# Layer planner: split window of 7 steps, longer estimate for small-row DMAs, eighth accumulator held back

## The chip, the core and the metric

The kernel runs on one core of a Trainium2 chip. The core has TensorE (matmuls and transposes, into the 8 banks of PSUM), VectorE, ScalarE and GpSimd (elementwise work), and DMA queues that are fed from SyncE, ScalarE and GpSimd. Each engine takes its instructions in the order of its own queue; semaphores hold an instruction until its inputs are there. In the profile PE is TensorE, DVE is VectorE, ACT is ScalarE, POOL is GpSimd and SP is SyncE. The metric is the device time of one execution in microseconds (us); lower is better.

## The reference

One encoder layer on 256 tokens of width 2048, all in float32: two kinds of attention side by side on one input projection, an output projection, and a gated feed-forward part of width 5632, with a layer norm at each seam.

```python
h = layer_norm(x, ln_in_g, ln_in_b)
proj = einsum('bsd,de->bse', h, w_in[l])                  # 2048 x 6144
na_out = neighbourhood_attention(na_q, na_k, na_v, na_rpb[l])   # 8 heads of 128
diff_out = differential_attention(d_q, d_k, d_v, lam, rel_bias_table)  # 4 heads of 256
diff_out = rms_norm(diff_out, diff_subln_g[l]) * (1.0 - lambda_init)
mixed = einsum('bse,ed->bsd', concatenate([na_out, diff_out]), w_out[l])
h = layer_norm(DEEPNORM_ALPHA * h + mixed, ln1_g[l], ln1_b[l])
ffn = einsum('bsf,fd->bsd', silu(h @ w_gate[l]) * (h @ w_up[l]), w_down[l])
h = layer_norm(DEEPNORM_ALPHA * h + ffn, ln2_g[l], ln2_b[l])
```

## The kernel before

**Units and splits.** Every weight matrix is read once, in units of 128 rows by 1024 columns (512 KB). A float32 product is made from three fast products: each operand is split into a high part (a copy to the `fp32r` type on ScalarE, `split_hi`, L406) and a low part (a subtraction on VectorE, `split_lo`, L410), and high x high, high x low and low x high are added in PSUM. So each unit costs ScalarE and VectorE one 128x1024 instruction each, and one slot of the 46 in the pool `slab` becomes two.

**Stages.** The units go in this order: six groups of 16 for the input projection (differential query, key, value, then neighbourhood query, key, value), two groups of 16 for the output projection (`o`, beginning with the rows of the differential attention), 16 units for one block of the gate and up matrices (`f`), ten groups of 16 for the rest of gate and up (`g`, `u`), and two groups of 44 for the down projection (`d`). For the first 144 units a *step* is one unit times one half of the tokens: six matmuls of 512 columns into two banks. `steps` (L1392) writes out the order. The first eight units of the input projection and of `f` are "whole" steps for the first half of the tokens: they multiply in float32 directly and need no split (two slower matmuls).

**Blocks of seven products.** From `g` on the work goes in blocks of two units by both token halves. A plain block has eight products (three matmuls each). A block listed in `SEVEN` or `SEVEN_D` (L38, L39) is done with seven products instead, from sums and differences of its parts, which are further work for VectorE and ScalarE (`seven_parts`, L1019; `add_mid_sums`, L1093). Seven products have seven accumulators; in the down projection a plain block has the accumulators 2, 3, 4 and 8, so both kinds together fill all eight banks. The product list of each block is in `products` (L1136); products 6 and 7 of a plain down block go to accumulator 8, and product 6 of a block of seven to accumulator 4.

**The planner.** The program is written out by a planner that runs when the kernel is built. `Timed` (L67) keeps an estimated clock for each engine and estimated times at which tiles are written and read; `note` (L98) adds each instruction's estimated cost. For a DMA issued on GpSimd it counts 1.05 us of issue, the transfer, and 1.2 + 2.0 us behind it. Work that is not a step of the main chain (layer norms, attention, the transposes of the gated result `mid_side`, L970) is a *side task*: a generator that yields the engine and the tiles that it wants next. In the main loop (L1535 to L1555), for each step:

- `load` issues weight loads up to 7 units ahead of the step's unit (8 in the blocks) on SP;
- the splits of the next `URGENT` = 3 steps are written out whatever they wait for;
- `side.elementwise` writes out side work for VectorE, ScalarE and GpSimd as long as that engine's clock is less than `BACKLOG` = 3 us past TensorE's;
- `next_part` writes out splits (and sums) for the units of the `window`, the next `AHEAD_S` = 24 steps, if their inputs are ready by the estimate, the engine is at most 2 us past TensorE, and slots are free (six more must stay free for units beyond the nearest);
- `side.best` puts side matmuls and transposes ahead of the step if their inputs and a bank have been ready for `SLACK` = 1.6 us by the estimate, or if the step is not `possible` yet.

An instruction, once written out, holds its place in its engine's queue, whatever the real times are.

**Around the change.** The neighbourhood attention loads a bias for each of its eight heads with four DMAs of 64 floats a row from GpSimd into a ring `nb` of two buffers (`na_bias`, L898); a `min` on VectorE takes it from there (`na_head`, L911) and frees the buffer. The same ring takes the transposed gated result: `mid_side` does four transposes into a bank, copies the bank to `nb` on ScalarE and stores that from GpSimd into `mid_d` in DRAM, from which the down projection reads it back. At the end of the last `u` group four such tasks are left. `take_product` (L1194) takes a bank for each accumulator when its first product comes; `Step.possible` (L1480) says when a step may go.

Of the kernel before, what the change touches and what calls it, by code (L numbers as in the profile page):

```python
# [35 lines left out]
NSG = 5  # L36
SLOTS = 46
SEVEN = (0, 2, 4, 6)  # L38
SEVEN_D = (range(0, 20, 3), range(20, 5, -3))  # L39
AGAIN = 3  # L40


class Engine:
# [21 lines left out]
class Timed:  # L65
# [32 lines left out]
    def note(self, name, op, outs, ins):  # L98
        n = max(int(np.prod([c for _, c in list(x.ap)[1:]])) for x in outs + ins)
        start = self.ready(*ins)  # L100
        for w, r, c in map(self.times, outs):
            start = max(start, float(r[c].max()), float(w[c].max()) if name != "pe" and op != "dma_start" else 0.0)
        if op == "dma_start":
            dims = [c for _, c in list(outs[0].ap)]
            rows = np.prod(dims[:-1])
            if name in self.clock:
                start = self.clock[name] = max(self.clock[name], start) + (1.05 if name == "pool" else 0.1)
            end = max(self.clock["dma"], start) + float(max(rows * dims[-1] * 4 / 360e3, rows * 0.0026))
            self.clock["dma"] = end
            end += self.LATENCY["dma"] + (2.0 if name == "pool" else 0.0)  # L110
            name = "dma"
        else:
            first = str(ins[0].dtype) if ins else ""
            wide = any("PSUM" in str(getattr(x.tensor, "_space", "")) for x in ins)
            m = int(np.prod([c for _, c in list(outs[0].ap)[1:]]))
            if name == "pe":
                if op == "transpose":
                    cost = 0.108
                elif first.endswith("float32"):
                    cost = m / 600 + 0.005  # L120
                else:
                    cost = m / 2400 + 0.0135
            elif name == "act":
                cost = 0.1 + n / 1200
            elif name == "dve":
                fast = op in ("tensor_scalar", "tensor_copy") and not wide
                cost = 0.07 + n / (1920 if fast else 960)
            else:
                cost = 0.1 + n / 400
            end = max(self.clock[name], start) + cost  # L130
        if name != "dma":
            self.clock[name] = end
            end += self.LATENCY[name]
        for w, r, c in map(self.times, ins):
            r[c] = np.maximum(r[c], end)
        for w, r, c in map(self.times, outs):
            w[c] = end
# [114 lines left out]
def layer_kernel(ctx: ExitStack, tc: tile.TileContext, A: dict, out: bass.AP):  # L252
# [39 lines left out]
    def used(key, n, *tiles):  # L292

        uses[key] = uses.get(key, 0) + 1
        if uses[key] == n:
            leave(*tiles)
# [31 lines left out]
    units = []  # L328
# [14 lines left out]
    hT, mixT, h1T, mid = {}, {}, {}, {}  # L343
# [13 lines left out]
    for n in range(2):  # L357
        ks = range(KF) if n == 0 else [k + i for k in range(KF - 2, -1, -2) for i in range(2)]
        add_group(("d", n), ks, [W_D[:, n * 1024 : (n + 1) * 1024]], mid, SEVEN_D[n])
    U = len(units)  # L360
# [6 lines left out]
    def splits_mid(u):  # L367


        g, k = units[u]["group"], units[u]["k"]  # L370
        return g == ("d", 0) and k % 4 == 0 or g == ("d", 1) and k % 4 == 2 and k // 4 < AGAIN

    def load(u):
# [11 lines left out]
        if splits_mid(u):  # L385
# [3 lines left out]
            nc.sync.dma_start(mid_whole[c], mid_d[c * P : (c + 1) * P, :])  # L389
        elif un["group"] == ("d", 1) and un["seven"] and un["k"] % 2 == 0 and un["k"] // 4 >= AGAIN:  # L390
            i = un["k"] // 2
# [24 lines left out]
    def tokens(x, t):  # L416

        return x[:, t] if len(x.shape) == 3 else x[:, t * P : (t + 1) * P]
# [42 lines left out]
    L2 = 8  # L461
    R0 = 3
    R1 = 8
    AHEAD = 7
# [47 lines left out]
    side = Side(nc, banks)  # L512
    have = {}
# [469 lines left out]
    def used_mid(c):  # L983
        n = 0 if ("mid 1", c) not in have else 1
        used(("mid", n, c), 1 + sum(i // 2 == c for i in SEVEN_D[n]), mid_whole[c])

# [106 lines left out]
    def add_mid_sums(u, parts):  # L1093

        i = units[u]["k"] // 2
        c = i // 2
        first = units[u]["group"][1] == 0 or c < AGAIN
        x = mid_whole[c][:, :, i % 2 * 2 : i % 2 * 2 + 2] if first else mid_pair[i]
# [37 lines left out]
    def products(u):  # L1136

        k = units[u]["k"]
        i = k // 2

        def x(row, t):
            return lambda: tuple(tokens(p, t) for p in units[u]["lhs"][k + row])

        def f(m):
            return lambda: forms[u if is_down(u) else i][m]

        def b(row, col):
            return lambda: w_block(u, row, col)

        def t13(m):  # L1150
            return lambda: (sums[u]["hi"][:, m], sums[u]["lo"][:, m])

        def t24(n):
            return lambda: (sums[u][2][:, n // 4], sums[u][4][:, n // 4])

        a_, b_, c_, d_ = x(0, 0), x(1, 0), x(0, 1), x(1, 1)
        if units[u]["seven"]:
            def b11():
                return sums[u]["b11"][:, 0], sums[u]["b11"][:, 1]

            return [
                (1, a_, b11),
                (2, b_, b(1, 0)),
                (3, f(2), b(1, 1)),
                (5, f(3), t13(0)),
                (7, f(0), t13(1)),
                (6, f(1), t24(2)),
                (4, d_, t24(4)),
            ]
        if is_down(u):  # L1170
            return [
                (2, a_, b(0, 0)),
                (2, b_, b(1, 0)),
                (3, a_, b(0, 1)),
                (3, b_, b(1, 1)),
                (4, c_, b(0, 0)),
                (4, d_, b(1, 0)),
                (8, c_, b(0, 1)),
                (8, d_, b(1, 1)),
            ]  # L1180
        return [
            (2, a_, b(0, 0)),
            (2, b_, b(1, 0)),
            (3, f(0), b(0, 1)),
            (3, f(1), b(1, 1)),
            (5, c_, b(0, 1)),
            (5, d_, b(1, 1)),
            (4, c_, b(0, 0)),
            (4, d_, b(1, 0)),
        ]  # L1190

    q, part, gate = {}, {}, {}

    def take_product(u, n):  # L1194
# [11 lines left out]
        if over:  # L1206
# [5 lines left out]
            if is_down(u):  # L1212
                if u in form_tiles:
                    leave(form_tiles[u])
                if name[1] == 1 and k % 4 == 0 or name[1] == 0 and k % 4 == 2 and k // 4 < AGAIN:
                    leave(*mid_tiles.pop(k // 4))
# [177 lines left out]
    def steps():  # L1394

        t1 = 0
        for u in range(SG):
            f = u < NF0 or FFN <= u < FFN + NF1  # L1400
            yield 0, u, f
            if f:
                continue
            if u < FFN - 40:
                behind = max(1, NF0 - (u - NF0) // R0)
            elif u < FFN:
                behind = max(1, L1 - (FFN - 1 - u) // 3) if u < FFN - 1 else 0
            else:
                behind = SG - 1 - u
            while t1 <= u - behind:  # L1410
                yield 1, t1, False
                t1 += 1
        for u in range(SG, U, 2):
            for n in range(4 if u >= U - L2 else len(products(u))):
                yield u, n

    def last_steps():
# [23 lines left out]
    def emit_part(o):  # L1441
        o["fn"]()
        o["done"] = True
# [16 lines left out]
    class Step:  # L1460
# [18 lines left out]
        def possible(self):  # L1479
            if self.kind == "product":  # L1480
                k = units[self.u]["k"]
                if is_down(self.u):

                    return ("mid", k // 4, 0) in have and (k > 2 or self.n < 6 or not side.tasks)
                return ("forms", k // 2) in have and all(("1", t, k // 4) in have for t in range(2))
            return possible(self.t, self.u, self.f)

# [47 lines left out]
    for i, step in enumerate(order):  # L1535
        step.load()
        window = order[i : i + AHEAD_S]
        for s in window[:URGENT]:
            s.finish_parts()
        coming = list(dict.fromkeys(p for s in window for p in s.parts if p[0] in raw and (not p[1] or p[0] + 1 in raw)))  # L1540
        near = {p for s in window[: AHEAD_N if step.kind == "product" else AHEAD] for p in s.parts}
        for _ in range(8):
            now = nc.clock["pe"]
            side.elementwise(now, BACKLOG)
            o = next_part(coming, near, now)
            while o is not None:
                emit_part(o)
                o = next_part(coming, near, now)
            task, when = side.best()
            main = nc.ready(*step.operands()) if step.possible() else 1e9  # L1550
            if task is None or when >= 1e8 or (when + SLACK > now and when + SLACK > main):
                break
            side.advance(task)
        step.operands()
        step.emit()  # L1555
# [45 lines left out]
```

## Time and profile before

| | before |
|---|---|
| time, median of 3 runs | 1139.98 us (1139.0 to 1140.16) |
| profiled execution: time | 1139.54 us |
| profiled execution: span | 1137.7 us |
| busy: TensorE | 1113.4 us (98%) |
| busy: TensorE weight load | 906.4 us (80%) |
| busy: VectorE | 932.1 us (82%) |
| busy: ScalarE | 601.2 us (53%) |
| busy: GpSimd | 60.3 us (5%) |
| mean granted clock of TensorE | 0.997 |
| DMA | 237.15 MB, mean 208 GB/s |

The span runs from the first to the last instruction; the time of the same execution is 1.84 us longer. All instructions carry the line of the helper that records them (L52), so they are told apart by their tiles: `sl` is a slot of the pool (weights, splits, activations), `acc` a bank of PSUM, `nb` and `s` are rings, `ident` is the identity for transposes. In a timeline the brackets show how long the engine stood idle before an instruction and what released it. A PE line `acc<-sl,sl` of 512 columns is a matmul of the main chain, `acc<-ident,...` is a transpose; a DVE or ACT line `sl<-sl` of 128x1024 is a split (in the blocks also a sum's). A few matmul records can be missing.

### The profile page before, as it was taken

The page shows a single profiled execution, that of the slowest core. Times are in us where ns is not written, and L with a number is a line of the kernel's source. Part 1 is how long each engine was busy: PE and PEld are TensorE (multiplying, and loading weights), DVE is VectorE, ACT ScalarE, POOL GpSimd, SP SyncE. Part 2 cuts the span into 40 slices and gives each one's busy share as a digit, 9 for nine tenths or more (in the row PEclk, how much of TensorE's full clock was granted, in tenths as well). Part 3 has the DMA queues.
Part 4 walks back from the last instruction along what each step waited for, and adds up shares of the span by engine and source line. Part 5 has one row for each costly group of instructions (what it writes and reads, how often), then busy time and mean ns, then how long its engine had stood idle before and what let it go on. Part 6 is the DMA issues. An engine that isn't in the chain of part 4 may idle for free.

```text
span 1137.7 us, 14161 instructions
## 1 busy us (share of the span) xinstructions
PE 1113.4 (98%) x5028; PEld 906.4 (80%) x5028; DVE 932.1 (82%) x1263; ACT 601.2 (53%) x781; POOL 60.3 (5%) x111
## 2 busy tenths in 40 slices
PE   8999999999899999999999999999999899999997
PEld 4788887887788876888888888888888788888885
DVE  7854856546774679989999999999999998799865
ACT  7344645525454337646646656556567556545630
POOL 2100003110100010000000000000000000000001
PEclk9999999999999999999999999999999999999999
DMA  9755457785756765665755755755756876758751
GB/s 352 223 169 171 145 163 146 229 146 179 152 174 216 239 201 188 211 215 185 245 200 184 261 202 169 276 202 172 272 208 225 278 246 265 224 202 311 253 167 74
DMA packets 70407, 237.15 MB, mean 208 GB/s; under 512 B 8516, under 2 KB 9924, under 8 KB 70336
## 3 DMA queue, kind: packets, MB, share of 16 engines
q1 hardware_dynamic: 65008, 220.49, 57.3%
q0 software_dynamic: 5168, 15.68, 6.9%
q8 instruction: 39, 0.64, 0.2%
q14 instruction: 32, 0.26, 0.1%
q10 hardware_dynamic: 160, 0.08, 0.0%
HBM read 226.25 MB, written 9.97 MB: 208 GB/s over the span
## 4 chain that ended last, share of the span: by engine, by line
issue 40%; PE 30%; DMA 3%; DVE 2%; POOL 1%; ACT 1%; POOLq 0%; SPq 0%; ACTq 0%; DVEq 0%
PE acc L52 30%; DMA nb<-in_na_rpb_dram 2%; DVE sl L52 1%; DMA sl<-in_w_in_dram 1%; POOL mid_d L52 1%; DMA mid_d<-nb 1%; ACT sl L52 1%; ACT s L52 0%; POOL h_d L52 0%; DVE stats L52 0%; POOL rstd L52 0%; DVE s L52 0%; POOLq L1597 0%; DVE mv L52 0%; ACT nb L52 0%
## 5 line engine op out<-in xcount | busy, mean ns | idle before, releaser
L52 PE MATMUL acc<-sl,sl 128*128 128x512 f32 (+1 forms) x4676 | 1064.9, 388 | 5.2 <-ACT nb L52 3.7
L52 PEld LDWEIGHTS acc<-sl,sl 128*128 128x128 f32 x4676 | 863.3, 188 | 186.9 <-issue 7.3
L52 DVE TENSOR_TENSOR sl<-sl,sl 128x1024 fp32r<-128x1024 f32 (+3 forms) x710 | 685.4, 1016 | 75.3 <-ACT sl L52 65.1
L52 ACT ACTIVATE sl<-sl 128x1024 fp32r<-128x1024 f32 (+1 forms) x530 | 502.7, 995 | 311.3 <-DVE sl L52 113.7
L52 DVE TENSOR_TENSOR sl<-acc,sl 128x256 fp32r<-128x256 f32 (+2 forms) x94 | 54.9, 596 | 42.2 <-ACT sl L52 31.1
L52 ACT ACTIVATE sl<-acc 128x256 fp32r<-128x256 f32 (+2 forms) x70 | 33.2, 496 | 70.7 <-PE acc L52 46.4
L52 DVE TENSOR_TENSOR sl<-sl 128x512 f32<-128x512 f32 (+1 forms) x76 | 41.4, 557 | 3.9 <-PE acc L52 3.1
L52 POOL DMA_DIRECT2D mid_d<-nb x22 | 11.9, 540 | 457.2 <-ACT nb L52 457.2
L52 ACT COPY nb<-acc 128x512 f32<-128x512 f32 x24 | 14.0, 588 | 35.3 <-PE acc L52 28.9
L52 ACT COPY sl<-acc 128x512 f32<-128x512 f32 x30 | 16.7, 590 | 23.3 <-PE acc L52 23.3
L52 ACT ACTIVATE s<-s 128x512 f32<-128x512 f32 x20 | 12.2, 631 | 25.5 <-DVE s L52 25.5
L52 POOL DMA_DIRECT2D nb<-in_na_rpb_dram x32 | 19.6, 621 | 88.8 <-DVE s L52 88.6
L52 PE MATMUL acc<-ident,s 128*128 128x128 f32 x136 | 20.6, 274 | 3.0 <-DVE s L52 2.9
L52 PEld LDWEIGHTS acc<-ident,sl 128*128 128x128 f32 x128 | 14.9, 141 | 10.7 <-issue 3.6
L52 PEld LDWEIGHTS acc<-ident,s 128*128 128x128 f32 x136 | 16.6, 140 | 8.0 <-issue 3.8
L52 DVE TENSOR_TENSOR sl<-sl,acc 128x512 f32<-128x512 f32 x16 | 10.6, 680 | 13.6 <-PE acc L52 13.5
L52 PE MATMUL acc<-ident,sl 128*128 128x128 f32 x128 | 18.0, 275 | 3.5 <-ACT sl L52 1.8
L52 ACT ACTIVATE s<-s,mx 128x256 f32<-128x256 f32 x32 | 15.9, 499 | 10.0 <-DVE mx L52 9.8
L52 DVE SCALAR_TENSOR_TENSOR sl<-sl,rstd,sl 128x512 f32<-128x512 f32 x22 | 16.5, 752 | 4.0 <-POOL rstd L52 3.1
L52 DVE BATCH_NORM_STATS2 stats<-sl 128x6 f32<-128x512 f32 x24 | 16.3, 691 | 3.0 <-DMA sl<-in_x_dram 2.4
L52 DVE TENSOR_TENSOR s<-nb,cap 128x256 f32<-128x256 f32 x16 | 6.2, 419 | 15.3 <-DMA nb<-in_na_rpb_dram 15.3
L52 DVE SCALAR_TENSOR_TENSOR sl<-sl,mv,sl 128x512 f32<-128x512 f32 x24 | 17.7, 746 | 0.3
(78 smaller groups left out, 212.6 us busy)
## 6 DMA issues: line engine op xcount, KB each, us to landing
sl<-in_w_in_dram SPq DMA_DIRECT2D x96, 512.0 KB, 4.7
sl<-in_w_down_dram SPq DMA_DIRECT2D x88, 512.0 KB, 5.8
sl<-in_w_gate_dram SPq DMA_DIRECT2D x80, 512.0 KB, 4.4
sl<-in_w_up_dram SPq DMA_DIRECT2D x80, 512.0 KB, 4.5
sl<-in_w_out_dram SPq DMA_DIRECT2D x32, 512.0 KB, 4.5
sl<-mid_d SPq DMA_DIRECT2D x14, 512.0 KB, 6.5
mid_d<-nb POOLq DMA_DIRECT2D x22, 256.0 KB, 3.4
sl<-in_w_gate_dram SPq DMA_DIRECT2D x16, 256.0 KB, 5.3
```

The costliest lines, as they stand in the source:

```text
L52: result = getattr(self.engine, op)(*args, **kw)
```

## The change

Three edits of the planner's rules and one of a list; the arithmetic of each product stays.

1. The `window` of the main loop is cut to 7 steps for steps that are not products; product steps further on, up to 24, stay in it.
2. The estimate behind a DMA issued on GpSimd becomes 8.0 instead of 2.0 us where the rows have fewer than 128 elements (the eight heads' bias loads, and two loads of constants in `setup`). Nothing but the planner's clock changes directly.
3. In the first group of the down projection the products 6 and 7 of plain blocks with k below 6 are taken out and put ahead of the first block that is not held back. `possible` changes with it: product 6 and later need the side tasks to be done only where accumulator 8 is not in use yet and the block is not one of seven.
4. The blocks of seven in that group become k/2 = 0, 4, 7, 10, 13, 16, 19 instead of 0, 3, 6, 9, 12, 15, 18; they stay seven in number.

```diff
-SEVEN_D = (range(0, 20, 3), range(20, 5, -3))
+SEVEN_D = ((0, 4, 7, 10, 13, 16, 19), range(20, 5, -3))
 AGAIN = 3
+WAITING = 6
...
-            end += self.LATENCY["dma"] + (2.0 if name == "pool" else 0.0)
+            end += self.LATENCY["dma"] + (0.0 if name != "pool" else 8.0 if dims[-1] < 128 else 2.0)
...
+        later = []
         for u in range(SG, U, 2):
-            for n in range(4 if u >= U - L2 else len(products(u))):
+            ns = range(4 if u >= U - L2 else len(products(u)))
+            if units[u]["group"] == ("d", 0) and units[u]["k"] < WAITING and not units[u]["seven"]:
+
+                later += [(u, n) for n in ns[6:]]
+                ns = ns[:6]
+            elif later:
+                yield from later
+                later = []
+            for n in ns:
                 yield u, n
...
-                    return ("mid", k // 4, 0) in have and (k > 2 or self.n < 6 or not side.tasks)
+                    return ("mid", k // 4, 0) in have and (
+                        8 in q or self.n < 6 or units[self.u]["seven"] or not side.tasks
+                    )
...
         window = order[i : i + AHEAD_S]
+        if step.kind != "product":
+            window = window[:AHEAD] + [s for s in window[AHEAD:] if s.kind == "product"]
```

## Rows read from the trace of the kernel before

**Rows 1.** The page's part 1: busy time, share of the span, instructions
```profile
PE 1113.4 (98%) x5028; PEld 906.4 (80%) x5028; DVE 932.1 (82%) x1263; ACT 601.2 (53%) x781; POOL 60.3 (5%) x111
```

**Rows 2.** Timeline of TensorE, 885 to 912: start us, us, what, xcount [idle before]
```profile
887.61 3.02 PE L52 MATMUL acc<-sl,sl 128*128 128x512 f32 x12
892.73 0.60 PE L52 MATMUL acc<-ident,s 128*128 128x128 f32 x4
896.99 15.29 PE L52 MATMUL acc<-sl,sl 128*128 128x512 f32 x59 [3.66 <-ACT nb L52]
```

**Rows 3.** Windows: busy of PE, PEld, DVE, ACT, POOL (xinstructions), PEclk, DMA, GB/s
```profile
306.19:316.19 10.00, 10.00 (x41) 8.13 (x42) 7.13 (x17) 5.87 (x12) 0.00 (x0) 0.83 0.35 122
896.99:906.99 10.00, 10.00 (x37) 8.07 (x38) 8.57 (x13) 8.35 (x10) 1.08 (x2) 0.83 0.58 212
906.99:916.99 10.00, 10.00 (x46) 8.29 (x45) 9.96 (x12) 6.59 (x9) 0.00 (x0) 1.00 0.80 248
```

**Rows 4.** Timeline of ScalarE, 885 to 900, and a piece of the chain
```profile
896.36 0.58 ACT L52 COPY nb<-acc 128x512 f32<-128x512 f32 x1 [4.66 <-DMA mid_d<-nb]
...
888.77 7.48 DMA mid_d<-nb
```

**Rows 5.** Groups on VectorE up to 894.6: line, what, xcount | busy, mean ns | idle
```profile
L52 DVE TENSOR_TENSOR sl<-sl,sl 128x1024 fp32r<-128x1024 f32 x353 | 413.7, 1218 | 61.9 <-ACT sl L52 59.1 <-issue 1.5
```

**Rows 6.** What VectorE waited for (us, times, longest); landing of the bias loads
```profile
DVE s L52 <- DMA nb<-in_na_rpb_dram: 15.3, 5, 4.8
...
DMA to landing us min/median/max: 5.0/9.2/14.6
```

**Rows 7.** Timelines of GpSimd, VectorE and TensorE, 280 to 322
```profile
290.01 2.44 POOL L52 DMA_DIRECT2D nb<-in_na_rpb_dram  x4 [0.32 <-DVE s L52]
...
305.15 0.43 DVE L52 TENSOR_TENSOR s<-nb,cap 128x256 f32<-128x256 f32 x1 [2.42 <-DMA nb<-in_na_rpb_dram]
...
306.19 0.72 PE L52 MATMUL acc<-ident,s 128*128 128x128 f32 x4 [2.93 <-DVE s L52]
```

**Rows 8.** Groups on VectorE and TensorE, up to 240, then up to 262.2
```profile
L52 DVE TENSOR_TENSOR sl<-sl,sl 128x1024 fp32r<-128x1024 f32 x75 | 89.0, 1219 | 21.5 <-ACT sl L52 21.0
...
L52 PE MATMUL acc<-sl,sl 128*128 128x512 f32 x816 | 190.0, 391 | 0.0
...
L52 DVE TENSOR_TENSOR sl<-sl,sl 128x1024 fp32r<-128x1024 f32 x86 | 102.0, 1219 | 30.9 <-ACT sl L52 30.4
...
L52 PE MATMUL acc<-sl,sl 128*128 128x512 f32 x912 | 211.8, 391 | 0.0
```

**Rows 9.** Timelines of ScalarE and TensorE, 222 to 272
```profile
262.32 1.06 ACT L52 ACTIVATE sl<-sl 128x1024 fp32r<-128x1024 f32 x1 [0.21 <-DMA sl<-in_w_in_dram]
...
263.92 0.66 PE L52 MATMUL acc<-ident,sl 128*128 128x128 f32 x4 [1.77 <-ACT sl L52]
265.29 0.66 PE L52 MATMUL acc<-ident,sl 128*128 128x128 f32 x4 [0.72 <-DVE sl L52]
```

**Rows 10.** Timeline of VectorE, 160 to 222
```profile
173.71 3.48 DVE L52 TENSOR_TENSOR sl<-sl,sl 128x1024 fp32r<-128x1024 f32 x3
```

**Rows 11.** What TensorE waited for (us, times, longest)
```profile
PE acc L52 <- DVE o L52: 2.5, 2, 1.5
```

**Rows 12.** Windows in the output projection's end and in the gate/up stretch
```profile
397.00:411.00 14.00, 14.00 (x63) 11.60 (x62) 7.65 (x8) 6.38 (x6) 0.00 (x0) 1.00 0.50 163
430.00:454.00 24.00, 22.47 (x90) 15.84 (x88) 23.86 (x47) 16.78 (x25) 0.54 (x1) 1.00 0.58 177
```

**Rows 13.** Groups on VectorE up to 430, then from 430 to 454
```profile
L52 DVE TENSOR_TENSOR sl<-sl,sl 128x1024 fp32r<-128x1024 f32 x135 | 161.0, 1220 | 57.5 <-ACT sl L52 56.2
...
L52 DVE TENSOR_TENSOR sl<-sl,sl 128x1024 fp32r<-128x1024 f32 x9 | 10.6, 1216 | 0.0
```

**Rows 14.** Timeline of TensorE, 398 to 512
```profile
436.93 4.38 PE L52 MATMUL acc<-sl,sl 128*128 128x512 f32 x18 [0.40 <-DVE sl L52]
442.41 29.81 PE L52 MATMUL acc<-sl,sl 128*128 128x512 f32 x130 [1.10 <-DVE sl L52]
```

## The prediction

> **What bounds the kernel now.** I read the busy shares first: TensorE works in 98% of the span [rows 1]. The change leaves its work alone (seven blocks with seven products stay seven), so only time in which TensorE stands still, or runs at half clock, can be won. Next its timeline, stage by stage, for the idle times in brackets and what ended them. Between the start and the last layer norm these count, each shown below with its rows: 3.66 us at the start of the down projection [rows 2], 2.93 in the neighbourhood attention, 2.5 in two waits in the differential attention, 1.77 and 0.72 at the end of the key projection, 0.40 and 1.10 in the gate/up stretch, 13.1 us in sum. Then the windows behind the two longest: there the granted clock averages 0.83 over 10 us, that is half of full speed (1.2 instead of 2.4 GHz) for a part, and the windows hold 41 and 37 matmuls where the next one holds 46 [rows 3]. Each of these two waits costs a further 0.17 x 10 = 1.7 us. The clock of the next window is 1.00 and gives 10 / 46 = 0.217 us a matmul: 0.65 us a product (three matmuls), 1.30 us a step (six).
>
> **The eighth accumulator.** Where the down projection starts, TensorE does four products, then transposes between single products, the fourth group at 892.73, then nothing until 896.99 [rows 2]. What released it is ScalarE's third copy out of PSUM, which had waited 4.66 us for a store that took 7.48 us, since the ring `nb` has two buffers [rows 4]. Why are all four transposes out by then? `possible` (L1484) lets product 6 of the first block go only when no side task is left, so the fourth group is forced out ahead of it. Six accumulators and two transposes hold all 8 banks, and product 6 needs the bank of the third copy. After the change the first block may go on (`units[...]["seven"]`). At 892.73 the one bank free is that of the second transposes, just emptied; with the 1.6 us of SLACK that the planner wants behind a free bank it should give this one to product 6 and keep the fourth transposes back until it believes the third copy done. The products of the eighth accumulator move behind 7 + 6 + 6 = 19 products, 12.4 us from 887.61, past 900, when the third copy (896.36) is long done. Saved: 3.66 + 1.7 = 5.4 us. The planner reckons some 5 us for that store, by its own constants (1.05 + 0.7 + 3.2), where 7.48 was measured, so the fourth transposes may be put ahead of their bank: 0 to 1.4 us given back. I take 0.7, the middle. Net 4.7.
>
> What the stop covered: VectorE had finished 353 splits of 128x1024 by 894.6 [rows 5], which is 344 for everything before the down projection (144 units, and ten groups of 20) and the 9 of blocks k = 0, 2 and 4, so the earlier start finds its operands. The next block, k = 6, no longer needs sums of its own on VectorE and ScalarE (they go to k = 8), which buys back the 5 us. Only TensorE's queue and those two see the move; the loads on SP keep their order.
>
> **Small-row DMAs.** VectorE waited 15.3 us, in five waits, for the bias loads (rows of 64 floats), whose landing takes 9.2 us from issue, 14.6 at most [rows 6]. The planner reckons 3.2 us behind the transfer, so it puts the `min` that reads them too early into VectorE's queue, and all behind it waits too. The dear case: loads issued from 290.01 on, `min` at 305.15 after 2.42 us of waiting, behind it the scaling of another head, and behind that TensorE's transposes, 2.93 us late [rows 7], plus 1.7 for the clock. With 9.2 reckoned the planner expects 4 x 1.05 + 0.7 + 9.2 = 14.1 us from the first issue; measured 15.1. The `min` then stands about where its data is due. Saved 4.6 us (0 to 4.6). The `min` also frees the buffer for the next head's loads on GpSimd's queue, so these start later and the eighth head ends perhaps 6 us later; that is hidden, for the output projection begins with the other attention's rows and wants the eighth head last. The other four waits were on no path to TensorE; they show in VectorE's lead: 75 units split at 240 where TensorE stood at unit (816 / 6 + 8) / 2 = 72, and 86 at 262 against (912 / 6 + 8) / 2 = 80 [rows 8].
>
> The Trainium skill, "DMA: Bandwidth & Descriptors", section "Anatomy of one DMA — SWDGE (gpsimd) path", fits 2.0 us + bytes / 436e3 to a load from this queue, an estimate of 2.2 us for 64 KB; by it the old figure was ample and this edit would bring 0 instead of 4.6. The trace's 9.2 us differ from it, and the sum goes by them.
>
> **Splits at most 7 steps ahead.** At 263.92 and 265.29 TensorE has waited 1.77 and 0.72 us to transpose the key projection [rows 9]. Its input is a copy on ScalarE directly behind a split that began at 262.32. With a lead of 6 units [rows 8] that split is for a unit some 12 steps away; under a cap of 7 steps, three and a half units, it is not in the queue. Saved 2.5 us (0 to 2.5). In the differential attention three splits in a row at 173.71 [rows 10] stand ahead of a chain of copies and scalings for which TensorE then waits 2.5 us in two pieces [rows 11]; perhaps one of the three is beyond the cap. I take half, 1.2 us (0 to 2.5).
>
> The price is the lead. In the last steps of the output projection VectorE is busy 7.65 of 14 us [rows 12] and uses the rest for gate/up units: 135 splits by 430 [rows 13], 7 more than the 128 units before them. The cap forbids these, since the steps that follow are eight whole-tile steps that need no split. They move, 7 x 1.18 = 8.3 us, into a stretch where VectorE is busy 23.86 of 24 us [rows 12], with 9 splits in 10.6 us [rows 13] and 13.3 us of other work, and where TensorE waits 0.40 and 1.10 us for it already [rows 14]. From 436.93 on twelve steps in a row each want a new unit: 14.2 us of splits in 12 x 1.30 = 15.6 us. If all other work stayed in front, the last split would end at 430 + 13.3 + 14.2 = 457.5 where it is wanted at 436.93 + 11 x 1.30 + 1.10 = 452.3: 5 us late, 6.7 with a clock drop. If the split wanted next always came first, even today's 1.5 us would go. The planner forces the parts of the next three steps and feeds VectorE no other work once that is 3 us behind; that is nearer to the second, so cost 1.5 us (-1.5 to 6.7). In the two attentions a shorter lead may let a burst on VectorE through to TensorE: nothing, or a wait of some 2 us like the one at 263.92 [rows 9] with a clock drop (1.7); I take 2.0 us, the middle (0 to 3.7). Slots are no concern: a split turns one slot into two, so later splits hold fewer, and SP's loads are not held up by them.
>
> **The sum.** -4.7 - 4.6 - 2.5 - 1.2 + 1.5 + 2.0 = -9.5 us. Against the profiled execution of 1139.54 that is 1130.0; the median of the runs stands 0.44 above it, so 1130.5. All gains at their best and no cost: 5.4 + 4.6 + 2.5 + 2.5 + 1.5 = 16.5, so 1123.5. The forecast's own range is 1125 to 1134.
>
> **Rivals.**
> 1. *The fourth transposes still go ahead of product 6.* It then waits for the third copy as now: 1130.5 + 4.7 = 1135. For it: the planner sends transposes out once their input has been ready for the SLACK, which may just have been so at 892.73. Against: its bank, too, must have been idle that long, and none had. Chance 0.10.
> 2. *The old reckoning of the bias loads was not the fault.* If they land late because they queue among weight loads, a later `min` meets the same lateness elsewhere and the 4.6 us stay: 1135. For it: landing spreads from 5.0 to 14.6 us [rows 6], which no constant follows. Against: the new one meets the dear case within 1 us. Chance 0.12. The skill's fit above would come to the same time.
> 3. *The change doesn't do what it says*: new waits appear where old ones go, as in 1 and 2 together and a little more, about 1139.5. Chance 0.07.
> 4. *Slower: VectorE runs out of lead.* Under the cap a burst of attention work on VectorE longer than 7 steps, 9.1 us, reaches TensorE. The lead stood 3 units lower at 240 than at 262 [rows 8], and the new one is 3.5. Priced at one unit short (2.6 + 1.7 us) in three bursts, 12.9, and the gate/up stretch at its worst, 6.7: 19.6 against gains of 13.0, so 1146.5. It decides once such waits pass 13 us together. Against it: loads still go out 7 units ahead, and the splits within the cap are queued ahead of each burst. Chance 0.10.
>
> The forecast keeps 0.61. About 0.2% (2.3 us) is what a measurement can tell from no change. Faster: 0.61 + 0.10 + 0.12 = 0.83; same 0.07; slower 0.10. The range reaches from 1125 to 1138; outside it are rivals 3 and 4 (0.17) and a little of the best case.
>
> **What would show it.** Right: between the last up product and the third block of the down projection no TensorE wait above 1.5 us, and a clock of 1.00; VectorE's waits for bias loads under 5 us in sum; no TensorE wait for copies at the end of the key projection; VectorE's splits before the second layer norm near 128, not 135, with TensorE's waits between 430 and 455 somewhat above 1.5 us. Wrong: a wait of some 3 us at product 6 as before; a wait of 3 us or more on `s` or `sl` in the attentions with a clock of 0.5 behind it; waits of 5 us or more on VectorE in the gate/up stretch.

## The result and the profile after

The changed kernel takes 1128.43 us (median of 4 runs, 1128.12 to 1129.68) against 1140.07 us for the kernel before beside it (4 runs, 1139.0 to 1140.8): ratio 0.9901 [0.9884, 0.9918], that is 11.6 us faster. Its profiled execution took 1128.12 us with a span of 1126.0 us. The forecast was 1130.5 us, faster, range 1125 to 1138.

The page's part 1 of the kernel after (busy us, share of the span, instructions):

```profile
PE 1110.7 (99%) x5028; PEld 903.8 (80%) x5028; DVE 929.1 (83%) x1263; ACT 596.9 (53%) x781; POOL 59.6 (5%) x111
```

Against [rows 1] nothing is missing but time: the same 5028 matmuls in a span 11.7 us shorter. The next fence holds every wait of TensorE over 0.15 us from its timeline, 30 to 1110 us, after (start us, us, engine, line, operation, tiles, xcount, [idle before <- releaser]):

```profile
182.30 0.94 PE L53 MATMUL acc<-ident,o 128*128 128x128 f32 x4 [0.60 <-DVE o L53]
289.74 0.72 PE L53 MATMUL acc<-ident,s 128*128 128x128 f32 x4 [1.51 <-DVE s L53]
309.49 0.72 PE L53 MATMUL acc<-ident,s 128*128 128x128 f32 x4 [0.23 <-DVE s L53]
428.41 1.66 PE L53 MATMUL acc<-sl,sl 128*128 128x512 f32 x6 [0.57 <-DVE sl L53]
432.22 30.88 PE L53 MATMUL acc<-sl,sl 128*128 128x512 f32 x133 [0.41 <-DVE sl L53]
888.42 0.66 PE L53 MATMUL acc<-ident,s 128*128 128x128 f32 x4 [0.52 <-ACT nb L53]
1004.19 1.46 PE L53 MATMUL acc<-sl,sl 128*128 128x512 f32 x4 [0.86 <-ACT sl L53]
1006.05 108.86 PE L53 MATMUL acc<-sl,sl 128*128 128x512 f32 x479 [0.40 <-DVE sl L53]
```

They add up to 5.10 us. Before, the waits that the prediction listed added up to 13.1, and two of them were followed by half clock for 1.7 us each [rows 3]. Now, in windows of the same kind (busy us of PE, PEld, DVE, ACT and POOL, then PEclk, DMA share, GB/s), the clock is full behind both places:

```profile
295.00:305.00 10.00, 10.00 (x53) 8.43 (x52) 7.79 (x19) 4.78 (x10) 0.00 (x0) 1.00 0.72 251
885.00:895.00 10.00, 9.48 (x44) 7.62 (x43) 9.67 (x12) 7.22 (x9) 1.08 (x2) 1.00 0.81 302
```

13.1 - 5.1 + 2 x 1.7 = 11.4 us. The two profiled executions differ by 1139.54 - 1128.12 = 11.4 us (their spans by 11.7). So nearly the whole gain lies in waits of TensorE and the clock behind them, and no other place has to be looked for.

By place: the start of the down projection went from 3.66 + 1.7 to 0.52 (4.8 us); the neighbourhood attention from 2.93 + 1.7 to 1.51 + 0.23 (2.9); the key projection from 2.49 to nothing (2.5); the differential attention from 2.5 to 0.60 (1.9); gate/up from 1.50 to 0.98 (0.5); and a wait of 1.26 at 1004, where the second down group begins, is new.

The start of the down projection, TensorE's timeline (answers to [rows 2]), then ScalarE's (to [rows 4]):

```profile
882.05 0.60 PE L53 MATMUL acc<-ident,s 128*128 128x128 f32 x4
882.41 0.94 PE L53 MATMUL acc<-sl,sl 128*128 128x512 f32 x3
883.18 0.60 PE L53 MATMUL acc<-ident,s 128*128 128x128 f32 x4
883.54 4.36 PE L53 MATMUL acc<-sl,sl 128*128 128x512 f32 x18
...
888.83 23.38 PE L53 MATMUL acc<-sl,sl 128*128 128x512 f32 x102
```

```profile
887.78 0.59 ACT L53 COPY nb<-acc 128x512 f32<-128x512 f32 x1 [4.50 <-DMA mid_d<-nb]
```

The third copy still waits 4.50 us for the store, as it did 4.66 before. But 18 matmuls (six products) now stand between the third and the fourth transposes, and TensorE waits only 0.52 us. Before, one product stood there, between 891.60 and 892.73:

```profile
891.95 0.94 PE L52 MATMUL acc<-sl,sl 128*128 128x512 f32 x3
```

### The profile page after: what moved, and what is told of

It is laid out like the page before. It is cut to its first block, busy times and chain, and to the rows that moved or that the text cites. A ratio compares the mean times of both kernels' runs of the same rounds, so it can differ in the third digit from the quotient of the medians.

```text
span 1126.0 us, 14140 instructions
## 1 busy us (share of the span) xinstructions
PE 1110.7 (99%) x5028; PEld 903.8 (80%) x5028; DVE 929.1 (83%) x1263; ACT 596.9 (53%) x781; POOL 59.6 (5%) x111
## 4 chain that ended last, share of the span: by engine, by line
PE 49%; issue 41%; DVE 5%; POOL 2%; ACT 2%; DMA 1%; POOLq 0%; DVEq 0%; ACTq 0%
PE acc L53 49%; DVE sl L53 3%; POOL mid_d L53 1%; ACT s L53 1%; DVE stats L53 1%; DVE s L53 1%; DMA mid_d<-nb 1%; ACT sl L53 1%; POOL rstd L53 0%; DMA nb<-in_ln_in_b_dram 0%; POOL h_d L53 0%; POOL rs L53 0%; ACT o L53 0%; DVE o L53 0%; ACT nb L53 0%
## 5 line engine op out<-in xcount | busy, mean ns | idle before, releaser
L53 DVE SCALAR_TENSOR_TENSOR sl<-sl,acc 128x512 f32<-128x512 f32 x10 | 6.8, 677 | 36.6 <-PE acc L53 36.6
L53 DVE TENSOR_SCALAR sl<-acc 128x512 f32<-128x512 f32 x8 | 5.5, 688 | 34.2 <-PE acc L53 34.2
L53 ACT ACTIVATE s<-s 128x512 f32<-128x512 f32 x20 | 12.3, 632 | 22.8 <-DVE s L53 22.8
L53 DVE TENSOR_TENSOR sl<-sl,acc 128x512 f32<-128x512 f32 x16 | 10.6, 680 | 12.3 <-PE acc L53 12.2
L53 PE MATMUL acc<-ident,sl 128*128 128x128 f32 x128 | 17.6, 273 | 0.5 <-DVE sl L53 0.4
```

The source lines that it names most:

```text
L53: result = getattr(self.engine, op)(*args, **kw)
```

## The experiments

Ratios are to the kernel before on the same chip; three chips were used, and it took 1137.6, 1138.8 and 1139.0 us on them. The change is called by its three parts: cap (edit 1), estimate (edit 2) and hold (edits 3 and 4). The diffs are against the changed kernel unless it is said otherwise.

| kernel | cap | estimate | hold | us | ratio |
|---|---|---|---|---|---|
| est_only | | x | | 1134.84 | 0.9960 [0.9946, 0.9975] |
| cap_only | x | | | 1130.98 | 0.9927 [0.9911, 0.9944] |
| no_hold | x | x | | 1131.30 | 0.9941 [0.9929, 0.9954] |
| no_cap | | x | x | 1131.59 | 0.9939 [0.9927, 0.9952] |
| no_est | x | | x | 1128.14 | 0.9909 [0.9894, 0.9924] |
| after_again | x | x | x | 1128.51 | 0.9904 [0.9884, 0.9923] |
| no_defer | x | x | part | 1129.52 | 0.9915 [0.9897, 0.9933] |
| hold_old_sevens | x | x | edit 3 | 1126.55 | 0.9896 [0.9883, 0.9910] |
| no_est_old_sevens | x | | edit 3 | 1126.31 | 0.9891 [0.9874, 0.9908] |
| best | x | x, and stores | edit 3 | 1127.19 | 0.9899 [0.9882, 0.9916] |
| cap_not_f | x, but for `f` | x | edit 3 | 1126.68 | 0.9897 [0.9879, 0.9915] |
| cap_until_80 | in part | | | 1135.51 | 0.9968 [0.9957, 0.9979] |

**The change once more, and the estimate alone and left out** (after_again, est_only, no_est).

> The changed kernel unaltered, beside the kernel before on the chip of the experiments, so that single edits can be set against both: 0.990 of the kernel before, about 1126.5 to 1128 us, with its 1.3 us of waits at the start of the second down group, sometimes with half clock behind them.

> The kernel before with the longer estimate for small rows alone. As predicted (4.6 us from the wait in the neighbourhood attention): 4.6 us faster, 1133 us. What the run without the cap suggests instead: the two waits at the end of the key projection (2.5 us) go too, since the bias loads' delay lies behind them, while some 2 us of wait with half clock stays in the neighbourhood attention; 3 to 4 us faster, about 1134 us.

```diff
-            end += self.LATENCY["dma"] + (2.0 if name == "pool" else 0.0)
+            end += self.LATENCY["dma"] + (0.0 if name != "pool" else 8.0 if dims[-1] < 128 else 2.0)
```

(est_only: this line alone, on the kernel before. no_est: this line alone put back.)

> The change without the longer estimate for small rows. Each edit on its own cause: VectorE waits some 15 us in sum for bias loads again (changed kernel 5.9), a TensorE wait of about 3 us in the neighbourhood attention comes back with half clock behind it, 4.6 us less the 1.7 us of small waits that the changed kernel has there: 1131 to 1133 us. Rival, the shorter window alone keeps VectorE's queue short enough: 1127.5 to 1129.5, no TensorE wait over 2 us there. By the fit of the Trainium skill (DMA: Bandwidth & Descriptors, Anatomy of one DMA) the old figure was ample, which would also give no change.

Alone, the estimate brings 0.4% of the 1%. With the cap in place it brings nothing that can be measured, in three pairs: 0.9941 against 0.9927, 0.9904 against 0.9909, 0.9896 against 0.9891, all with wide overlaps. The timelines of TensorE and VectorE, est_only, in the neighbourhood attention:

```profile
297.47 0.72 PE L53 MATMUL acc<-ident,s 128*128 128x128 f32 x4 [1.89 <-DVE s L53]
...
301.28 0.75 DVE L53 TENSOR_TENSOR s<-nb,cap 128x256 f32<-128x256 f32 x2
304.82 0.75 DVE L53 TENSOR_TENSOR s<-nb,cap 128x256 f32<-128x256 f32 x2
```

The eighth head's `min` now stands at 304.82, 17.6 us behind its loads (issued from 287.23), and waits for nothing; the estimate does what it was said to do. But TensorE still waits 1.89 us for `s` in the same stretch, for another reason, which the same place of no_cap shows best. VectorE's timeline there:

```profile
292.64 2.35 DVE L53 TENSOR_TENSOR sl<-sl,sl 128x1024 fp32r<-128x1024 f32 x2
294.91 0.42 DVE L53 TENSOR_TENSOR sl<-acc,sl 128x256 fp32r<-128x256 f32 x1
295.77 0.42 DVE L53 TENSOR_TENSOR sl<-acc,sl 128x256 fp32r<-128x256 f32 x1 [0.45 <-ACT sl L53]
296.75 0.17 DVE L53 RECIPROCAL sums<-sums 128x2 f32<-128x2 f32 x1 [0.55 <-ACT s L53]
296.95 0.62 DVE L53 TENSOR_SCALAR s<-s,sums 128x256 f32<-128x256 f32 x2
```

Two splits in a row, 2.35 us, stand ahead of the chain of small instructions that ends with the scaled rows of `s`. ScalarE, whose part of that chain comes behind this copy, had waited for VectorE as well:

```profile
295.36 0.38 ACT L53 ACTIVATE sl<-acc 128x256 fp32r<-128x256 f32 x1 [3.70 <-DVE sl L53]
```

**Without the cap, without the hold, and the cap alone** (no_cap, no_hold, cap_only).

> The change without the 7-step window; the other edits stay. Each edit on its own cause: the waits of some 1.8 and 0.7 us at the end of the key projection and of some 2.5 us in the differential attention come back, the gate/up stretch waits 1.5 us where the changed kernel waits 1.0: some 4 us slower than the changed kernel, about 1132.5 us. Rival, one common cause (late bias loads made the weight loads and with them the far splits late): with the longer estimate kept, those waits stay away and the time stays within 1 us of the changed kernel, 1127.5 to 1129.5.

> The change without the held-back products, the new rule for product 6 and the moved blocks of seven. Theory: the wait of 3.66 us at product 6 comes back with 1.7 us of clock behind it, and the 1.3 us of waits at 1004 to 1006 us, at the start of the second down group, go: 5.4 - 0.5 - 1.3, so 3.5 us slower than the changed kernel, about 1132 us. Rival, the earlier start only runs into VectorE later: within 1 us of the changed kernel.

> The kernel before with the 7-step window alone. As predicted, 3.7 us of gain less 3.5 of price: no change, 1137.5 us, the 2.9 us wait in the neighbourhood attention with half clock stays. What the run without the longer estimate suggests instead: the cap alone clears the key projection, most of the neighbourhood attention and half of the differential attention, 9 to 10 us less 1.5 of small waits: 7 us faster or more, 1129 to 1131 us.

```diff
-        if step.kind != "product":
-            window = window[:AHEAD] + [s for s in window[AHEAD:] if s.kind == "product"]
```

(no_cap: these lines out. cap_only: these lines alone on the kernel before. no_hold: edits 3 and 4 put back.)

The cap alone brings 7.8 of the 10 to 11 us. TensorE's waits up to 880, cap_only:

```profile
181.90 0.94 PE L53 MATMUL acc<-ident,o 128*128 128x128 f32 x4 [0.58 <-DVE o L53]
289.32 0.72 PE L53 MATMUL acc<-ident,s 128*128 128x128 f32 x4 [1.50 <-DVE s L53]
427.75 2.46 PE L53 MATMUL acc<-sl,sl 128*128 128x512 f32 x8 [0.57 <-DVE sl L53]
431.56 30.89 PE L53 MATMUL acc<-sl,sl 128*128 128x512 f32 x133 [0.42 <-DVE sl L53]
```

Without the longer estimate, the 2.93 us wait with its half clock is gone, and so are the waits at the key projection. Left out, it lets 1.55 us at 184.75 and 1.90 at 297.45 (clock 0.83 over 295 to 305) come back, but not the waits at 264: those go with either edit.

The hold is what clears the down projection. TensorE's timeline, no_hold, then the window around it:

```profile
883.60 0.94 PE L53 MATMUL acc<-sl,sl 128*128 128x512 f32 x3
884.37 0.60 PE L53 MATMUL acc<-ident,s 128*128 128x128 f32 x4
888.86 6.43 PE L53 MATMUL acc<-sl,sl 128*128 128x512 f32 x21 [3.89 <-ACT nb L53]
```

```profile
885.00:895.00 10.00, 6.14 (x21) 4.98 (x22) 8.61 (x14) 5.32 (x7) 1.08 (x2) 0.83 0.84 312
```

The fourth transposes are out after one product and the wait of [rows 2] is back, with the clock at 0.83; in cap_only it is 3.86 us and 0.66 over the same window, in est_only 3.29 us and 0.66 over 890 to 900.

**The hold in parts** (no_defer, hold_old_sevens).

> The changed kernel without the held-back list: products 6 and 7 of blocks k = 2 and 4 stay in their places, the new rule for product 6 and the moved blocks stay. If holding back is needed, product 6 of block k = 2 comes 13 products (8.5 us) after the first one of the group, before the bank of the fourth copy is empty (about 12 us after it in the changed kernel): a wait of 2 to 3.5 us on ScalarE's copy, 2 to 5 us slower than the changed kernel. If the new rule for product 6 alone does it: no wait over 1 us there and the changed kernel's time.

> The change with the old list of blocks of seven (k/2 = 0, 3, 6, ... 18); products held back as in the change. If moving the blocks is what pays for the earlier start, VectorE is late with the sums of block k = 6 and TensorE waits there, up to 5 us: 1129 to 1132 us. Rival, VectorE's lead is enough there and the move only crowds the end: no wait at k = 6, none at the start of the second down group (1.3 us in the changed kernel), about 1127 us.

```diff
-            if units[u]["group"] == ("d", 0) and units[u]["k"] < WAITING and not units[u]["seven"]:
-                later += [(u, n) for n in ns[6:]]
-                ns = ns[:6]
-            elif later:
-                yield from later
-                later = []
```

(no_defer: these lines out. hold_old_sevens: `SEVEN_D` as before.) The rule for product 6 alone leaves 0.29 and 0.86 us of waiting at 888 and 891, with no half clock: it does most, and the held-back products are worth about 1 us (1129.5 against 1128.5), within the intervals. The moved blocks of seven bring nothing. With the old list no wait appears at k = 6, and the 1.26 us at 1004 is gone: 1126.55 us against 1137.62 on its chip (0.9896; its four runs, 1126.14 to 1126.89, lie below the eight of the change, 1127.96 to 1129.68, though these were taken on other chips).

**What is left to gain there** (best, no_est_old_sevens, cap_not_f). All three have the old blocks of seven.

> The change with the blocks of seven of the kernel before (0, 3, 6, ...), and the estimate behind the stores of the gated result raised from 2.0 to 5.5 us, so that the planner reckons about the 7.5 us measured for such a store. Theory (the fourth transposes go ahead of their bank because the store is reckoned too short): the wait of 0.5 to 0.9 us for ScalarE's copy at 888 is gone, no new wait at the next blocks, ratio 0.9892, some 0.5 us below the old sevens alone (0.9896). Rival (late stores in the estimate hold the transposes of the other fifteen blocks back too, so the gated result comes later): a new wait for sl or acc in the last u group or at k = 4 to 8 of the down projection, ratio 0.990 to 0.992.

```diff
-            end += self.LATENCY["dma"] + (0.0 if name != "pool" else 8.0 if dims[-1] < 128 else 2.0)
+            slow = dims[-1] < 128 or "mid_d" in outs[0].tensor.name
+            end += self.LATENCY["dma"] + (0.0 if name != "pool" else (8.0 if dims[-1] < 128 else 5.5) if slow else 2.0)
```

> The cap and the held-back products with the old blocks of seven, without the longer estimate for small rows. Theory (with the cap in place the longer estimate brings nothing): ratio 0.9890 to 0.9900, no wait of over 2 us for s between 285 and 310, VectorE's waits for bias loads some 9 us as in the earlier run without the estimate. Rival (the estimate is worth its 2.9 us wait once the rest is calm): a wait of 2 to 3 us for s with half clock behind it, ratio 0.992 to 0.994.

> The change with the old blocks of seven, and with the units of the block of gate and up between the output projection and the second layer norm left outside the cap, so these may be split up to 24 steps ahead again. By the prediction (the cap costs 1.5 us there, for it moves seven splits into a stretch where VectorE is full): 1.5 us faster than the old sevens alone, ratio 0.9883. Rival (the first such splits are wanted in the order of the steps anyway, and the early ones stand ahead of side work): the waits of 0.40 and 1.09 us for sl are back in place of 0.57 and 0.41, ratio 0.990, 0.5 us slower.

```diff
-            window = window[:AHEAD] + [s for s in window[AHEAD:] if s.kind == "product"]
+            window = window[:AHEAD] + [s for s in window[AHEAD:] if s.kind == "product" or units[s.u]["group"][0] == "f"]
```

In best the fourth transposes go after 33 matmuls and wait for nothing, as the theory has it, but another wait appears, in neither of its theories. TensorE's timeline, best:

```profile
883.09 7.77 PE L53 MATMUL acc<-sl,sl 128*128 128x512 f32 x33
890.70 0.60 PE L53 MATMUL acc<-ident,s 128*128 128x128 f32 x4
...
1003.59 110.05 PE L53 MATMUL acc<-sl,sl 128*128 128x512 f32 x483 [0.93 <-ACT sl L53]
```

This is the place at which the change itself waits 1.26 us, and here the sevens are the old ones. So the moved sevens are one way to bring this wait about, not its only cause. ScalarE's timeline at that place, after:

```profile
1003.51 1.58 ACT L53 ACTIVATE sl<-sl 128x512 fp32r<-128x512 f32 x2 [6.30 <-DVE sl L53]
```

ScalarE had waited 6.30 us for VectorE, which empties the first group's accumulators then and makes the sums for the next block of seven behind that. Whether that block's sums are ready turns on a microsecond in VectorE's queue. It took back what best had won: 0.9899 against 0.9896.

no_est_old_sevens shows again that the estimate can go (1126.31 us, the lowest median of all, not to be told apart from hold_old_sevens). cap_not_f has the waits of the kernel before at 428 and 434, 0.40 and 1.11 us, in place of 0.57 and 0.41, and comes to 0.9897: the cap costs nothing in that stretch.

**Where the cap acts on the bias loads** (cap_until_80): the kernel before with the cap, but only up to unit 79.

> The kernel before with the cap alone, and that only for steps of units below 80, so not in the neighbourhood value projection, the output projection and after. Theory 1 (local: the splits for units far ahead, queued on VectorE while the biased rows are made, push the min and the scaling of the heads back): a TensorE wait of 2 to 3 us for s between 290 and 310 comes back with a clock near 0.83 behind it, ratio 0.996 to 0.997. Theory 2 (history: what the cap changes before, the times of the weight loads and of the bias loads among them, has already moved the heads): no such wait, ratio 0.992 to 0.994 as with the cap throughout. Either way the waits at 264 stay away, and the splits by the second layer norm are 135 with waits of 0.40 and 1.09 near 430 to 440.

```diff
+        if step.kind != "product" and step.u < 80:
+            window = window[:AHEAD] + [s for s in window[AHEAD:] if s.kind == "product"]
```

GpSimd's, VectorE's and TensorE's timelines, cap_until_80, then the window behind the wait:

```profile
281.57 4.87 POOL L53 DMA_DIRECT2D nb<-in_na_rpb_dram  x8 [43.15 <-DVE s L53]
...
296.00 0.42 DVE L53 TENSOR_TENSOR s<-nb,cap 128x256 f32<-128x256 f32 x1
299.79 0.42 DVE L53 TENSOR_TENSOR s<-nb,cap 128x256 f32<-128x256 f32 x1 [3.37 <-DMA nb<-in_na_rpb_dram]
...
300.73 1.16 PE L53 MATMUL acc<-ident,s 128*128 128x128 f32 x4 [3.62 <-DVE s L53]
```

```profile
300.73:310.73 10.00, 10.00 (x42) 8.28 (x43) 7.71 (x17) 7.02 (x13) 0.00 (x0) 0.86 0.40 132
```

And GpSimd's and VectorE's, cap_only:

```profile
284.20 2.44 POOL L53 DMA_DIRECT2D nb<-in_na_rpb_dram  x4 [0.32 <-DVE s L53]
...
297.81 0.75 DVE L53 TENSOR_TENSOR s<-nb,cap 128x256 f32<-128x256 f32 x2
```

The wait is back, 3.62 us, so it is the cap in this stretch that removes it, not what it does before. The reason given with that theory is wrong, though: the far splits don't push the `min` back, the `min` comes too early for its data. Counted from the issue of the eighth head's loads, VectorE reaches the second half of its `min` after 12.7 us before (290.01 to 305.15 - 2.42) and after 12.4 us here (284.0, the middle of the eight issues, to 296.42), and has to wait; the data are there 15.1 and 15.8 us after the issue. With the longer estimate it comes 17.6 to 18.5 us after the issue, behind its data. In cap_only it comes after 13.6 us, still too early for 15.1; but there the loads land sooner. The landing of the eighth head's four loads, each from its own issue, before and then in cap_only:

```profile
DMA to landing us min/median/max: 7.8/12.4/13.5
...
DMA to landing us min/median/max: 7.2/9.8/10.5
```

The last of the four was issued at 286.0 there, so the data were in at 296.5, 12.3 us after the first issue. (In cap_until_80 the slowest took 13.9 us, in no_est, which also has the cap throughout, 10.3.) So the estimate cures this case by putting more work ahead of the `min`, and the cap by loads that land some 3 us sooner; why they do so was not tried.

## Why the prediction was right

The time, the sign and the eighth accumulator were right. Of the rest of the sum several terms were credited to the wrong edit, and errors of both signs met; that the sum came so near is in part luck.

**The eighth accumulator** (-4.7 forecast). Right by its own steps: product 6 takes the bank, the fourth transposes go ahead of theirs by 0.52 us, where 0 to 1.4 was said and 0.7 taken, and the clock stays at 1.00. The place gained 3.66 + 1.7 - 0.52 = 4.8 us. With the old sevens the edit is worth 4 to 5 us (0.9941 to 0.9896, 0.9927 to 0.9891). The step that failed is the last sentence of that part: the move of a block of seven from k = 6 to k = 8 doesn't buy back 5 us, for nothing was missing there, and the change has a wait at the next group, which the prediction didn't look at. The two pairs of runs put the cost of the move at 0.9 us (0.9904 against 0.9896) and 2.0 us (0.9909 against 0.9891), both within the intervals.

**Small-row DMAs** (-4.6). The place gained what was said (2.93 + 1.7 gone), but not by this edit. The step that failed is "saved 4.6" itself: it took the late `min` for the only thing that could hold TensorE there. With the estimate alone that wait goes, but one of 1.89 us comes at the transposes of the head before, behind two splits; with the cap alone the 2.93 us wait goes too, though the estimate is the old one. The two edits meet in the same microseconds, so their savings don't add. Rival 2 held half of the truth: under the new figure the waits of VectorE for bias loads do move elsewhere (10.9 us in three with est_only, 15.3 in five before [rows 6]), though the dear one goes. After, they are these (VectorE's waits: us, times, longest):

```profile
DVE s L53 <- DMA nb<-in_na_rpb_dram: 5.9, 2, 3.1
```

5.9 us, where under 5 was named; with the cap alone they are 9.4 us in four. The rule of the Trainium skill, "DMA: Bandwidth & Descriptors", section "Anatomy of one DMA — SWDGE (gpsimd) path", would have left this edit without effect. Beside the cap it has none that can be measured, but not for that reason: the slowest of the eighth head's loads land 10.3 to 13.9 us after their issue (above), not 2.2, and the edit does move the `min`.

**The cap.** Key projection (-2.5): the waits are gone, as said, and ScalarE's copy no longer stands behind a split (timeline of ScalarE, after; compare [rows 9]):

```profile
256.95 0.60 ACT L53 ACTIVATE sl<-acc 128x512 f32<-128x512 f32 x1 [3.74 <-PE acc L53]
```

But they go with the estimate alone too, where the copy (at 260.36) still has a split in front, at 259.39. ScalarE's splits wait for their weights there in both kernels, but in est_only they come some 3 us sooner (258.13 and 259.39, before 261.05 and 262.32), with TensorE no further ahead, and 7.66 MB came in between 225 and 265 us, against 6.60. So the lateness of the loads was part of it, and "the other four waits were on no path to TensorE" is doubtful; why the loads come sooner there was not tried. Differential attention (-1.2): 1.9 measured, within 0 to 2.5. Gate/up (+1.5): the waits fell from 1.50 to 0.98 us, -0.5, within -1.5 to 6.7 but of the other sign. VectorE's group of splits up to 418 us, after, beside the 135 of [rows 13]:

```profile
L53 DVE TENSOR_TENSOR sl<-sl,sl 128x1024 fp32r<-128x1024 f32 x128 | 150.4, 1219 | 25.9 <-ACT sl L53 24.4
```

The seven splits do move, 128 as forecast. The window of 24 us is as full as before (answer to [rows 12]):

```profile
421.00:445.00 24.00, 22.95 (x87) 15.16 (x85) 23.90 (x40) 20.33 (x28) 0.54 (x1) 1.00 0.41 135
```

Both ends of the term were worked out rightly; the choice between them was not. The low end, "if the split wanted next always came first", is nearer to what happens, and the idle time that VectorE used earlier on bought no lead that TensorE needed. Attention bursts (+2.0): 1.51 and 0.23 us, and no clock drop behind them, so 1.7: right, and cap_only and cap_until_80 show that the 1.5 us comes with the cap in that stretch.

**By edit**, then: cap 7.8 us alone and 4.0 beside the other two, 0.9939 against 0.9904 (forecast 0.2 net); hold 4 to 5 with the old sevens and 1 to 2 less with the new (4.7); estimate 4.0 alone and nothing measurable beside the cap (4.6). Cap and estimate together (no_hold) bring 6.3 us, not 7.8 + 4.0. The sum came out near because the cap's unforeseen gain stands in the same place as the estimate's foreseen one. **Rival 4**, VectorE out of lead, fell: no burst costs more than 1.51 us.

## What to carry to other kernels

Where several waits of one queue overlap, a saving belongs to a place, not to an edit: price each edit alone and beside the others, since two remedies for one wait don't add. An instruction that needs nothing soon still costs when it stands ahead of one that is wanted, so a short look-ahead in an in-order queue can be worth more than a better estimate of when data come. And ahead of moving work to "make room", ask whether anything was late there: the part of this change that did so brought nothing and seems to have cost 1 to 2 us.

## What had not been expected of the hardware

Loads in small rows take much DMA time. In the 40 us from 270 to 310, after, the two kinds of queue (packets, MB, share of the 16 engines):

```profile
q1 hardware_dynamic: 1581, 5.75, 41.6%
q0 software_dynamic: 256, 0.52, 26.6%
```

The second is the eight bias loads: 0.52 MB in rows of 256 bytes take 0.266 x 40 = 10.6 us of all engines by the time of their packets, some 49 GB/s, where the first moves 5.75 MB in 16.6 us, some 346 GB/s. That fits the late landing of the eight, up to 12.1 us from issue in this stretch; whether they hold up each other or the weights beside them was not tried.

Half clock can follow quite short waits, not always. The same two waits of 0.86 and 0.40 us at the second down group left the clock at full speed in one execution of the change and at half for a part in another; the window 1005 to 1010 of the change, first its profiled run and then that of after_again:

```profile
1005.00:1010.00 5.00, 4.60 (x19) 3.46 (x20) 5.00 (x5) 2.86 (x5) 0.00 (x0) 1.00 0.98 305
```

```profile
1005.00:1010.00 5.00, 4.60 (x13) 3.31 (x13) 5.00 (x5) 2.74 (x4) 0.00 (x0) 0.66 0.90 304
```

19 matmuls in the one and 13 in the other; these two executions took 1128.12 and 1129.58 us. The waits of some 1.5 us at 289 show no such drop: the clock over 289 to 299 is 1.00 in all ten profiled executions that have the cap in that stretch. But the 1.90 us of no_cap and the 1.89 us of est_only, at the same place, again differ; their windows:

```profile
295.00:305.00 10.00, 8.10 (x36) 6.62 (x35) 8.28 (x21) 7.85 (x17) 0.00 (x0) 0.83 0.68 163
```

```profile
295.00:305.00 10.00, 8.11 (x44) 6.65 (x43) 8.29 (x22) 7.84 (x16) 0.00 (x0) 1.00 0.79 180
```

What a drop costs differs as well. Behind the wait for the store at the down projection it was 0.17 x 10 = 1.7 us in no_hold (0.83) and 0.34 x 10 = 3.4 us in cap_only and est_only (0.66), so the 1.7 us that the prediction put on each drop is one of two sizes seen.
